# A two-layer trunk on one core: filter spectra from even and odd samples, transposes ahead of feed-forward stretches, modulation loads spread anew

## The chip, the cores and the metric

One core of one Trainium2 chip runs the whole program, in fp32. The metric is device time in microseconds (us) of one execution. TensorE (PE, with its weight loads as PEld), VectorE (DVE), ScalarE (ACT), GpSimd (POOL) and SyncE (SP, which issues nearly all DMAs here) each take their instructions in program order.

## The reference

256 latent tokens and 256 context tokens of width 2048 pass two layers. Layer 0 mixes with attention (differential and windowed heads), layer 1 with a Hyena long convolution; each is followed by a gated feed-forward with 5632 hidden columns.

```python
m = s_lat @ ada_w[l] + ada_b[l]                       # modulation: six vectors of 2048 a layer
sh1, sc1, g1, sh2, sc2, g2 = jnp.split(m, 6, axis=-1)
h = _rms(xs, norm1_g[l]) * (1.0 + sc1) + sh1
y = attention(h, hc, w_in, w_out) if l % 2 == 0 else _hyena(h, hw_in, filters, hw_out)
xs = xs + g1 * y
xs = xs + g2 * _conv_ffn(_rms(xs, norm2_g[l]) * (1.0 + sc2) + sh2, w_gate, w_val, conv_w, conv_b, w_down)

def _hyena_filters(...):                              # a small net of position: 2 orders x 2 directions x 2048
    a = jnp.sin(freq * (z @ f_w0 + f_b0)); a = jnp.sin(freq * (a @ f_w1 + f_b1)); a = jnp.sin(freq * (a @ f_w2 + f_b2))
    return (a @ f_w3).reshape(L, 2, 2, D) * decay     # the convolution then works on their spectra
```

## The kernel before

Every product of two fp32 matrices is done as three fp32r products. A weight tile of 128x2x512 fp32 (512 KB) is loaded by SP (`wload`, lines 323 to 326, a ring of six), ACT rounds it to a high part (L331), DVE subtracts to get the low part (L332, a ring of three each), and `products` (L335 to L341) issues high x high, low x high and high x low. A weight tile makes 24 matmuls of 256 columns where the activations are the moving side. `mm3` (L343 to L346) does the same for one product.

The program is one long list of stages. The start computes the first modulation vectors with PE (`ada_block`, L896 to L917, products L905), the norms of both inputs, the filter network, the filters and their spectra for the first half of the 2048 filter columns, and the first of five key/value projections. Then come the other four (KV), four query projections with attention running beside them (Q), the out-projection, feed-forward 0 (FFN0: eleven chunks of 512 hidden columns upward, each 16 weight tiles and 384 matmuls, and then two halves of eight output tiles downward), the Hyena stage, its out-projection, and FFN1.

The other modulation vectors are no PE work: class `Ada` (L454 to L498) loads a tile of 512 KB (L470, ring of six, SP) and DVE multiplies and sums it (L480). There are 320 such loads. They run in the background of the stages: `drive` (L312 to L321) calls for so many of them per step of a stage, at rates that a table of constants sets (L180 to L188), unless the flag `calm` is set. A step is one weight tile in most stages. `need` issues what is missing of a vector before its use.

Background generators do the filters in the same way: `filter_net` (L525 to L556) is the network of three layers, `filters` (L558 on) takes 512 filter columns at a time: `samples` multiplies the network's last activations by the third layer's weights (L578, plain fp32), by the decay (DVE), and sums absolute values for the normalisation; `spectra` multiplies by a table of cosines and sines in fp32r (L344 to L346) and ACT copies the result out (L604). Columns 0 to 1023 are done in the start; columns 1024 to 1535 are filling in the out-projection and in the norm's gap ahead of FFN0; the last 512 fill the second half of FFN0's down projection and the gap ahead of the Hyena stage. `GAP = 3, 5` is how many of the filling's steps are kept for the two gaps. In such a gap PE waits for a chain: sums of squares (L376), scale (L378), a Newton step on DVE and POOL (L350 to L372), a diagonal on ACT (L384), a product that spreads it (L385), and the modulated activations (L417).

## Time and profile before

| | us |
|---|---|
| three runs | 2664.08, 2691.29, 2657.86 (median 2664.08) |
| the profiled execution | 2660.88, span of its instructions 2659.0 |
| PE, PEld, DVE, ACT busy in the span | 2556.5, 2361.2, 1924.1, 1267.6 |
| first key/value stage after the start begins | 187.5 |
| FFN0 begins, its down part, the Hyena stage | 698.8, 1215.6, 1484.3 |
| FFN1 begins in earnest, ends | 1932.8, 2654.4 |

A view by windows gives, for each stretch, how long each engine was busy, the clock that TensorE was granted as a share of full speed, the busy share of the 16 DMA engines and what they moved. A row of the waits says who waited for what, for how long in total, how many times and the longest. A row of the timeline has start, duration, engine, line and operation; in brackets the idle time before it and what ended that.

### The profile page before, as it was taken

Reading aid. Unit: us, or ns where it says so; the run is one execution under the profiler, and the core shown is the slowest. Engines: PE = TensorE matmul, PEld = TensorE weight load, DVE = VectorE, ACT = ScalarE, POOL = GpSimd, SP = SyncE. Lnnn points to the kernel's source line nnn. Section 1 sums busy time; section 2 is a strip of 40 time slices with the busy share of each in tenths; the row PEclk is TensorE's granted clock in tenths of the full one; section 3 lists DMA queues with packets and bytes.
Section 4 is the critical chain, followed back from the end, with each engine's and each line's share of the span. In section 5 each row is a group of like instructions: output and inputs, shape, how many; then the busy total and the mean of one; then the engine's idle time right before and its main releaser. Section 6 shows DMA issues by size and latency. Waiting matters only on the chain.

```text
span 2659.0 us, 48167 instructions
## 1 busy us (share of the span) xinstructions
PE 2556.5 (96%) x19526; PEld 2361.2 (89%) x19526; DVE 1924.1 (72%) x2911; ACT 1267.6 (48%) x1820; POOL 37.6 (1%) x146
## 2 busy tenths in 40 slices
PE   6999998899899999999999999998999999999999
PEld 2568886678899999989999999998899999999999
DVE  5446668768898888889777678889875555556664
ACT  3452235655644443445444655554454444445543
POOL 0000000100000000000000000000000000000000
PEclk8999999999999999999999999999999999999999
DMA  8876676448799998899897665556766666666664
GB/s 293 318 267 216 213 242 232 161 151 263 242 354 327 337 342 326 316 331 344 296 309 247 202 201 170 179 176 214 253 206 193 194 193 195 194 193 196 192 211 137
DMA packets 177158, 639.99 MB, mean 241 GB/s; under 512 B 19783, under 2 KB 19880, under 8 KB 176936
## 3 DMA queue, kind: packets, MB, share of 16 engines
q1 hardware_dynamic: 174632, 628.53, 70.8%
q10 hardware_dynamic: 2304, 8.39, 0.8%
q8 instruction: 153, 2.51, 0.4%
q14 instruction: 69, 0.57, 0.1%
HBM read 624.25 MB, written 12.58 MB: 239 GB/s over the span
## 4 chain that ended last, share of the span: by engine, by line
PE 74%; DMA 9%; DVE 8%; issue 4%; ACT 4%; POOL 1%; SPq 0%; ACTq 0%; POOLq 0%; DVEq 0%
PE ps_proj L340 22%; PE ps_hy L340 9%; PE ps_kv L340 7%; PE ps_ada L340 2%; DVE araw_ada L480 2%; PE ps_q L340 1%; PE ps_ada L905 1%; DVE wlo_proj L332 1%; PE ps_attn L838 1%; PE ps_filters L578 1%; PE ps_attn L815 1%; PE ps_conv L344 1%; PE ps_conv L345 0%; PE ps_ffn1.0_3359_20701 L340 0%; PE ps_conv L346 0%
## 5 line engine op out<-in xcount | busy, mean ns | idle before, releaser
L332 DVE TENSOR_TENSOR wlo_proj<-raw_proj,whi_proj 128x1024 fp32r<-128x1024 f32 x240 | 292.3, 1221 | 145.9 <-ACT whi_proj L331 143.8
L331 ACT CAST whi_proj<-raw_proj 128x1024 fp32r<-128x1024 f32 x240 | 251.5, 1053 | 301.7 <-PE ps_proj L340 261.8
L480 DVE SCALAR_TENSOR_TENSOR araw_ada<-araw_ada,slB 128x1024 f32<-128x1024 f32 x320 | 388.9, 1217 | 0.0
L340 PE MATMUL ps_proj<-ph,whi_proj 128*128 128x256 f32 x1408 | 196.2, 279 | 0.4 <-ACT ph L349 0.3
L340 PE MATMUL ps_proj<-ph,wlo_proj 128*128 128x256 f32 x1408 | 192.9, 278 | 0.0
L340 PE MATMUL ps_proj<-pl,whi_proj 128*128 128x256 f32 x1408 | 192.8, 278 | 0.0
L340 PEld LDWEIGHTS ps_proj<-ph,whi_proj 128*128 128x128 f32 x1408 | 175.9, 188 | 4.2 <-ACT whi_proj L331 1.6
L340 PEld LDWEIGHTS ps_proj<-pl,whi_proj 128*128 128x128 f32 x1408 | 175.3, 188 | 0.0
L340 PEld LDWEIGHTS ps_proj<-ph,wlo_proj 128*128 128x128 f32 x1408 | 175.2, 188 | 0.0
L331 ACT CAST whi_hy<-raw_hy 128x1024 fp32r<-128x1024 f32 x96 | 101.3, 1056 | 105.7 <-PE ps_hy L340 82.2
L332 DVE TENSOR_TENSOR wlo_hy<-raw_hy,whi_hy 128x1024 fp32r<-128x1024 f32 x96 | 116.5, 1222 | 47.6 <-ACT whi_hy L331 46.6
L340 PE MATMUL ps_hy<-hhi,whi_hy 128*128 128x256 f32 x768 | 108.8, 281 | 1.2 <-ACT hhi L417 1.2
L340 PE MATMUL ps_hy<-hlo,whi_hy 128*128 128x256 f32 x768 | 106.0, 279 | 0.2 <-DVE hlo L419 0.2
L340 PE MATMUL ps_hy<-hhi,wlo_hy 128*128 128x256 f32 x768 | 104.5, 279 | 0.0
L340 PEld LDWEIGHTS ps_hy<-hhi,whi_hy 128*128 128x128 f32 x768 | 99.1, 189 | 3.7 <-ACT hhi L417 1.7
L340 PEld LDWEIGHTS ps_hy<-hlo,whi_hy 128*128 128x128 f32 x768 | 96.9, 188 | 1.0 <-DVE hlo L419 0.4
L340 PEld LDWEIGHTS ps_hy<-hhi,wlo_hy 128*128 128x128 f32 x768 | 95.8, 189 | 0.1
L332 DVE TENSOR_TENSOR wlo_kv<-raw_kv,whi_kv 128x1024 fp32r<-128x1024 f32 x40 | 48.8, 1222 | 60.6 <-ACT whi_kv L331 60.5
L331 ACT CAST whi_kv<-raw_kv 128x1024 fp32r<-128x1024 f32 x40 | 42.0, 1052 | 100.3 <-PE ps_kv L340 89.9
L340 PE MATMUL ps_kv<-whi_kv,hhi 128*128 128x512 f32 x256 | 66.0, 400 | 0.0
L340 PE MATMUL ps_kv<-wlo_kv,hhi 128*128 128x512 f32 x256 | 64.2, 393 | 0.0
L340 PE MATMUL ps_kv<-whi_kv,hlo 128*128 128x512 f32 x256 | 64.0, 393 | 0.0
(9816 smaller groups left out, 7652.9 us busy)
## 6 DMA issues: line engine op xcount, KB each, us to landing
araw_ada<-ada_t SPq DMA_DIRECT2D x320, 512.0 KB, 4.8
raw_proj<-wd SPq DMA_DIRECT2D x176, 512.0 KB, 4.5
raw_hy<-hw_in SPq DMA_DIRECT2D x96, 512.0 KB, 3.8
raw_ada<-ada_w SPq DMA_DIRECT2D x46, 512.0 KB, 6.6
raw_kv<-w_in SPq DMA_DIRECT2D x40, 512.0 KB, 3.8
raw_q<-w_in SPq DMA_DIRECT2D x32, 512.0 KB, 4.4
raw_proj<-w_out SPq DMA_DIRECT2D x32, 512.0 KB, 4.8
raw_proj<-hw_out SPq DMA_DIRECT2D x32, 512.0 KB, 4.5
```

The costliest lines, as they stand in the source:

```text
L331: A.copy(hi, raw)
L332: V.tensor_tensor(lo, raw, hi, op=ALU.subtract)
L340: PE.matmul(o, ll if p == 2 else lh, rl if p == 1 else rh, start=first and p == 0, stop=last and p == 2, skip_group_check=True)
L344: PE.matmul(o, lh, rh, start=first, stop=False, **kw)
L480: V.scalar_tensor_tensor(out=raw, in0=raw, scalar=1.0, in1=slB[:, h * 1024:(h + 1) * 1024], op0=ALU.mult, op1=ALU.mult, accum_out=acc[:, h ...
L578: PE.matmul(p, src[:, tt * P:(tt + 1) * P], w3[:, o], start=True, stop=True)
L815: PE.matmul(s, qT[:, h % 4, q_], KTb[:, hb // 4], start=True, stop=True)
L838: PE.matmul(o[:, 0:P], wT[:, kt * P:(kt + 1) * P], v, start=kt == 0, stop=kt == 3)
L905: PE.matmul(pv[32 * q:32 * q + 32], sl[:, 2 * i + q], raws[q // 2][:, q % 2], start=i == 0, stop=i == 6, tile_position=(0, 32 * q))
```

## The change

Five edits.

1. The cosine and sine table is halved. Samples stand in the order even, then odd; `spectra` makes one product from the even samples and one from the odd ones and gets a frequency and its mirror from their sum and difference: six matmuls of 512 columns for a half instead of twelve, one ACT copy and two DVE steps instead of two ACT copies. It yields once per half where it yielded twice.
2. `samples` uses `mm3` on the split activations and split third-layer weights (two more tiles, `w3s`) instead of an fp32 matmul.
3. In the start three steps of the filter work run before the first norm step and three behind it, the filters are stepped at 2.0 and then 1.0 instead of 1.2, and banks 2 and 3 go from the norms to the filters during the first block.
4. `turn`: four transposes of the identity into the first bank of a stretch, ahead of chunks 1 and 5 and of each down half in both feed-forwards.
5. The rates of modulation loads.

```diff
-START_RATE = 1.2
+START_RATE = 2.0, 1.0
-KV_ADA, Q_ADA, O_ADA, HY_ADA, HO_ADA = 1.3, 1.0, 0.8, 0.5, 0.6
-F0_ADA, F1_ADA = (0.9, 0.5), (0.4, 0.2)
+KV_ADA, Q_ADA, O_ADA, HY_ADA, HO_ADA = 1.9, 0.7, 0.8, 0.45, 0.6
+F0_ADA, F1_ADA = (0.7, 0.6), (0.4, 0.2)
...
+    def turn(bank):
+
+        for i in range(4):
+            PE.transpose(bank[:, i * P:(i + 1) * P], ident, ident)
...
-            a = s2([m, T]) if i < 2 else keep([P, T], "fa")
+            a = s2([m, T])
...
-        am = keep([P, T], "fam")
-        V.tensor_copy(am[:HW], a[:HW])
-        V.tensor_scalar(am[HW:], a[HW:], -1.0, None, op0=ALU.mult)
-        layers.extend((a, am))
+        for src in range(2):
+            if src:
+                V.tensor_scalar(a[HW:], a[HW:], -1.0, None, op0=ALU.mult)
+            hi, lo = (keep([P, T], f"fa{n}{src}", F32R) for n in "hl")
+            split(hi, lo, a)
+            layers.append((hi, lo))
...
-                    PE.matmul(p, src[:, tt * P:(tt + 1) * P], w3[:, o], start=True, stop=True)
+                    t = slice(tt * P, (tt + 1) * P)
+                    mm3(p, sh[:, t], sl_[:, t], w3[0][:, o], w3[1][:, o], True, True)
...
-                for f in range(2):
-                    p = ftag[0]()
-                    for tt in range(2):
-                        c = slice(half * T + f * P, half * T + (f + 1) * P)
-                        mm3(p, fh[:, tt, c], fl[:, tt, c], xh[:, tt], xl[:, tt], tt == 0, tt == 1)
-                    A.activation(so[:, f], p, AF.Copy, scale=1.0 / (2 * T))
-                    yield
+                c = slice(half * P, (half + 1) * P)
+                pe, po = ftag[0](), ftag[0]()
+                mm3(pe, fh[:, 0, c], fl[:, 0, c], xh[:, 0], xl[:, 0], True, True)
+                mm3(po, fh[:, 1, c], fl[:, 1, c], xh[:, 1], xl[:, 1], True, True)
+                e = s2([P, 512], F32, "se")
+                A.activation(e, pe, AF.Copy, scale=1.0 / (2 * T))
+                V.scalar_tensor_tensor(out=so[:, 0], in0=po, scalar=1.0 / (2 * T), in1=e, op0=ALU.mult, op1=ALU.add)
+                V.scalar_tensor_tensor(out=so[:, 1], in0=po, scalar=(half * 2 - 1) / (2 * T), in1=e, op0=ALU.mult,
+                                       op1=ALU.subtract if half else ALU.add)
+                yield
...
-            if not spare:
-                yield
+            w3s = [q4([P, 2, 512], F32R, "w3s") for _ in range(2)]
+            split(*w3s, w3)
+            yield
...
-    AD, ST = Ring(4, 5), Ring(0, 1, 2, 3)
-    ftag[0] = Ring(6, 7)
+    AD, ST = Ring(4, 5), Ring(0, 1)
+    ftag[0] = Ring(6, 7, 2, 3)
...
-    bg.one()
+    for _ in range(3):
+        bg.one()
     norm_bg.one()
+    for _ in range(3):
+        bg.one()
...
-            bg.step(START_RATE)
+            bg.step(START_RATE[g > 0])
...
             norm_bg.drain()
+            ftag[0] = Ring(6, 7)
...
                 banks = rings[half].four()
+                if n > 3:
+                    turn(banks[0])
...
             banks = ring.four()
+            if ch in (1, 5):
+                turn(banks[0])
```

Line numbers of the kernel after the change lie 8 to 23 higher: its L343 is L340 of before, L347 to L349 are L344 to L346, L384 and L393 are L376 and L385, L478 is L470, L328 is L325, L547 is L539, L920 is L905.

By stage the 320 modulation loads stand in SP's order as follows, before and after: start 2 and 5, KV 31 and 45, Q 34 and 29, with a few between the stages; out-projection 25 and 24; FFN0 up 160 and 119, FFN0 down 43 and 53; Hyena stage 1 and 2, its out-projection 15 and 14; FFN1 7 and 28.

PE's order at the beginning of the program, before: two layers of the filter network (`ps_filters`), then the first modulation products (`ps_ada`) and the sums of squares of the first norm (`ps_nx`).

```order
L539 MATMUL ps_filters_140<-s_116,u_118 64x256
L539 MATMUL ps_filters_166<-s_151,s_120 64x256
L905 MATMUL ps_ada_37_131<-raw_ada_38_132,sl 32x512 x2
L905 MATMUL ps_ada_37_131<-raw_ada_39_134,sl 32x512 x2
L376 MATMUL ps_nx_185<-ones_67,sq_153 128x1 x8
L905 MATMUL ps_ada_37_131<-raw_ada_46_158,sl 32x512 x2
L905 MATMUL ps_ada_37_131<-raw_ada_47_160,sl 32x512 x2
L539 MATMUL ps_filters_229<-s_177,s_120 128x256
```

And after the change, where `w3s` and `fah` are split parts of the third layer's weights and of the network's result:

```order
L547 MATMUL ps_filters_123<-s_116,u_118 64x256
L547 MATMUL ps_filters_136<-s_134,s_120 64x256
L547 MATMUL ps_filters_157<-s_147,s_120 128x256
L920 MATMUL ps_ada_60_195<-raw_ada_61_196,sl 32x512 x2
L920 MATMUL ps_ada_60_195<-raw_ada_62_198,sl 32x512 x2
L920 MATMUL ps_ada_60_195<-raw_ada_73_231,sl 32x512 x2
L920 MATMUL ps_ada_60_195<-raw_ada_74_233,sl 32x512 x2
L347 MATMUL ps_filters_208<-w3s_191,fah_171 128x512
```

The third layer of the network and the first samples have moved ahead of half of the first modulation products and of the first norm.

PE's order at the end of the gap ahead of FFN0, before: the last of the filling (`ps_fill`, 25 matmuls stand between the last square sum and L385), the product that spreads the norm, and the first product of FFN0.

```order
L346 MATMUL ps_fill_6001<-fhl_5661,fl_5474 128x512
L344 MATMUL ps_fill_6001<-fhl_5661,fh_5473 128x512
L345 MATMUL ps_fill_6001<-fhl_5662,fh_5473 128x512
L346 MATMUL ps_fill_6001<-fhl_5661,fl_5474 128x512
L385 MATMUL ps_proj_1288_5977<-s_5978,ones_67 128x128 x2
L340 MATMUL ps_ffn0.0_1297_6029<-hhi_6010,whi_ffn0.0_1302_6035 128x256
```

And after, where the square sums (L384) and the first group of transposes (L354) stand there:

```order
L384 MATMUL ps_proj_1312_6002<-ones_67,sq_5939 128x1
L384 MATMUL ps_proj_1312_6002<-ones_67,sq_5966 128x1
L384 MATMUL ps_proj_1312_6002<-ones_67,sq_5969 128x1
L354 MATMUL ps_ffn0.1_1392_6621<-ident_66 128x128 x4
L393 MATMUL ps_proj_1317_6030<-s_6031,ones_67 128x128 x2
L343 MATMUL ps_ffn0.0_1322_6055<-hhi_6036,whi_ffn0.0_1327_6061 128x256
```

The filling has moved ahead of the square sums, and the transposes written ahead of chunk 1 stand ahead of chunk 0. In layer 1 they stand still earlier, between the two halves of the last pass of the Hyena out-projection.

SP's order in FFN0's up part, before: a load of a modulation tile (`araw_ada`) nearly behind every weight tile (`raw_ffn0`).

```order
L325 DMA raw_ffn0.3_1518_7714<-wg 128x1024
L470 DMA araw_ada_7744<-ada_t 128x1024
L325 DMA raw_ffn0.3_1522_7747<-wv 128x1024
L470 DMA araw_ada_7777<-ada_t 128x1024
L325 DMA raw_ffn0.3_1526_7780<-wg 128x1024
L470 DMA araw_ada_7810<-ada_t 128x1024
```

And after, where some weight tiles follow each other:

```order
L328 DMA raw_ffn0.3_1541_7782<-wg 128x1024
L478 DMA araw_ada_7711<-ada_t 128x1024
L328 DMA raw_ffn0.3_1545_7815<-wv 128x1024
L328 DMA raw_ffn0.3_1550_7854<-wg 128x1024
L478 DMA araw_ada_7749<-ada_t 128x1024
L328 DMA raw_ffn0.3_1553_7884<-wv 128x1024
```

About two modulation loads have moved out for every ten weight tiles.

## Rows read from the trace of the kernel before

**Rows 1.** The page's first part: busy us and share of each engine.

```profile
PE 2556.5 (96%) x19526; PEld 2361.2 (89%) x19526; DVE 1924.1 (72%) x2911; ACT 1267.6 (48%) x1820; POOL 37.6 (1%) x146
```

**Rows 2.** Windows by stage, with the line that names the columns.

```profile
core 0: us, PE busy (x) PEld busy (x) DVE busy (x) ACT busy (x) POOL busy (x), PEclk, DMA share, GB/s
0.00:60.00 60.00, 36.36 (x137) 16.57 (x138) 33.84 (x91) 20.30 (x31) 4.62 (x26) 0.86 0.92 324
60.00:187.40 127.40, 123.05 (x589) 73.71 (x588) 55.96 (x137) 68.27 (x137) 0.00 (x0) 0.97 0.79 292
187.50:369.60 182.10, 182.10 (x811) 147.92 (x809) 111.42 (x169) 47.45 (x72) 7.01 (x30) 1.00 0.64 208
684.90:698.80 13.90, 10.78 (x56) 8.76 (x54) 9.46 (x22) 6.31 (x14) 3.78 (x10) 1.00 0.80 262
698.80:744.00 45.20, 45.20 (x384) 45.20 (x385) 42.42 (x72) 27.84 (x43) 0.00 (x0) 0.96 0.83 299
744.00:831.10 87.10, 87.10 (x771) 87.10 (x770) 77.99 (x115) 39.80 (x48) 0.00 (x0) 1.00 0.96 348
831.10:1215.60 384.50, 364.25 (x3075) 356.91 (x3074) 321.48 (x460) 161.69 (x194) 0.00 (x0) 1.00 0.92 330
1215.60:1330.30 114.70, 114.70 (x1013) 114.60 (x1012) 98.46 (x117) 64.00 (x69) 0.00 (x0) 1.00 0.89 313
1927.80:1994.20 66.40, 62.61 (x524) 62.32 (x525) 51.04 (x85) 37.73 (x59) 1.57 (x8) 0.92 0.64 206
1932.80:2654.40 721.60, 721.52 (x6336) 720.92 (x6336) 426.56 (x497) 344.71 (x412) 0.00 (x0) 1.00 0.63 192
```

**Rows 3.** Windows of line 340's matmuls on PE: us, busy (count), clock.

```profile
1220.00:1330.00 110.00, 110.00 (x973) 1.00 0.89 311
1332.00:1395.00 63.00, 63.00 (x538) 1.00 0.92 318
```

**Rows 4.** Waits of SP's queue in FFN0, 831.1 to 1215.6: us, times, longest.

```profile
SPq L470 <- DVE araw_ada L480: 238.5, 99, 5.2
```

**Rows 5.** Timeline of PE in the gap ahead of the Hyena stage.

```profile
1476.48 0.39 PE L345 MATMUL ps_fill<-fhl,fh 128*128 128x512 f32 x1
...
1478.75 0.39 PE L345 MATMUL ps_fill<-fhl,fh 128*128 128x512 f32 x1
```

**Rows 6.** Groups of PE's instructions, 0 to 190 us: the fp32 samples.

```profile
L578 PE MATMUL ps_filters<-w,fa 128*128 128x512 f32 x16 | 10.9, 768 | 3.9 <-DMA w<-f_w 3.9
L578 PE MATMUL ps_filters<-w,fam 128*128 128x512 f32 x16 | 10.5, 742 | 0.0
```

**Rows 7.** Timeline of DVE, then PE, in the gap ahead of FFN0.

```profile
689.20 1.22 DVE L480 SCALAR_TENSOR_TENSOR araw_ada<-araw_ada,slB 128x1024 f32<-128x1024 f32 x1
...
690.41 1.22 DVE L480 SCALAR_TENSOR_TENSOR araw_ada<-araw_ada,slB 128x1024 f32<-128x1024 f32 x1
...
696.88 0.78 PE L385 MATMUL ps_proj<-s,ones 128*128 128x128 f32 x4 [1.97 <-ACT s L384]
```

**Rows 8.** Timeline of PE around two groups of transposes (L1211).

```profile
1679.62 0.60 PE L1211 MATMUL ps_conv<-ident,fold 128*128 128x128 f32 x4
1679.98 1.18 PE L340 MATMUL ps_hy<-hhi,whi_hy 128*128 128x256 f32 x8
1680.99 1.07 PE L340 MATMUL ps_hy<-hlo,whi_hy 128*128 128x256 f32 x8
1681.90 1.07 PE L340 MATMUL ps_hy<-hhi,wlo_hy 128*128 128x256 f32 x8
...
1765.33 0.60 PE L1211 MATMUL ps_conv<-ident,fold 128*128 128x128 f32 x4
...
1766.71 1.11 PE L340 MATMUL ps_hy<-hlo,whi_hy 128*128 128x256 f32 x8
1767.65 1.11 PE L340 MATMUL ps_hy<-hhi,wlo_hy 128*128 128x256 f32 x8
```

**Rows 9.** The page's costliest groups: a third of the Hyena projection's products.

```profile
L340 PE MATMUL ps_hy<-hhi,whi_hy 128*128 128x256 f32 x768 | 108.8, 281 | 1.2 <-ACT hhi L417 1.2
```

More of the change, by code (lines that the diff above doesn't have):

```diff
@@ L144, in constants @@
     n = 2 * L
-    fo = np.concatenate([np.arange(0, L, 2), np.arange(1, L, 2)])[None, :]
+    fo = np.concatenate([np.arange(0, L, 2), L - 1 - np.arange(0, L, 2)])[None, :]
     t = np.arange(L)[:, None]
-    ph = np.pi * ((t * (2 * fo + 1)) % (2 * n)) / n
-    fmat = np.concatenate([np.cos(ph), np.sin(ph)], axis=1).reshape(2, P, 512).transpose(1, 0, 2).reshape(P, 1024)
+    eo = np.concatenate([np.arange(0, L, 2), np.arange(1, L, 2)])
+    ph = np.pi * ((eo[:, None] * (2 * fo[:, :P] + 1)) % (2 * n)) / n
+    fmat = np.concatenate([np.cos(ph), np.sin(ph)], axis=1).reshape(2, P, 2 * P).transpose(1, 0, 2).reshape(P, 512)
     th = np.pi * (((2 * t[:P] + 1) * (2 * fo + 1)) % (4 * n)) / (2 * n)
@@ L165, in constants @@
     return {
-        "k_tab": tab, "k_fg": fg, "k_z": np.ascontiguousarray(z.T),
-        "k_decay": np.ascontiguousarray(decay.reshape(2, P, D).transpose(1, 0, 2)),
+        "k_tab": tab, "k_fg": fg, "k_z": np.ascontiguousarray(z[eo].T),
+        "k_decay": np.ascontiguousarray(decay[eo].reshape(2, P, D).transpose(1, 0, 2)),
     }
@@ L561, in filters @@
             return
-        fh, fl = (t.rearrange("p (t f) -> p t f", t=2) for t in split_const(0, 1024, "f"))
+        fh, fl = (t.rearrange("p (t f) -> p t f", t=2) for t in split_const(0, 512, "f"))
         w3v = f_w3.rearrange("w (o d c) -> w o d c", o=2, d=2)
@@ L575, in samples @@
                 ab = []
-                for i, src in enumerate(layers):
+                for i, (sh, sl_) in enumerate(layers):
                     p = ftag[0]()
-                    PE.matmul(p, src[:, tt * P:(tt + 1) * P], w3[:, o], start=True, stop=True)
+                    t = slice(tt * P, (tt + 1) * P)
+                    mm3(p, sh[:, t], sl_[:, t], w3[0][:, o], w3[1][:, o], True, True)
                     h = s2([P, 512], F32, "hf")
@@ L617, in filters @@
             SP.dma_start(dec, k_decay[:, :, dc * 512:(dc + 1) * 512])
-            if not spare:
-                yield
+            w3s = [q4([P, 2, 512], F32R, "w3s") for _ in range(2)]
+            split(*w3s, w3)
+            yield
             for o in range(2):
                 hl = [q4([P, 2, 512], F32R, "fhl") for _ in range(4)]
-                yield from samples(o, dc, w3, dec, hl)
+                yield from samples(o, dc, w3s, dec, hl)
                 if spare and before:
@@ L1166, in trunk_kernel @@
         SP.dma_start(xsp[:, 4 * g:4 * g + 4], xs[g])
-    dh, dl = split_const(1024, 512, "d")
-    ih, il = split_const(1536, 512, "i")
+    dh, dl = split_const(512, 512, "d")
+    ih, il = split_const(1024, 512, "i")
     zb = keep([P, 48], "zb")
```

## Prediction

> **What bounds the kernel now.** The page's first part comes first: TensorE (PE) is busy 96% of the span [rows 1], so an engine average can't tell where time is to be had, and the next view is the table of windows by stage [rows 2]. Its columns are busy times per engine, the granted clock (1.00 is the 2.4 GHz level), the DMA share and GB/s. Four kinds of stage stand out. The start (0 to 187.5 us) has PE at 36.36 of its first 60 us and 123.05 of the next 127.40, with transfers at 324 and 292 GB/s: both limits are near. The KV projections run with PE at 182.10 of 182.10 us and 208 GB/s: pure PE. The up part of layer 0's feed-forward (FFN0) from chunk 3 on (831.1 to 1215.6) moves 330 GB/s at a DMA share of 0.92 with holes in PE. The whole of FFN1 (1932.8 to 2654.4) is PE at 721.52 of 721.60 us with 192 GB/s.
>
> How long would those stretches be with nothing in the way? The view of one line's matmuls [rows 3] gives it: inside an undisturbed stretch 973 products of 128x256 take 110.00 us, 113.05 ns each, and a little later, after a short stall at 1330.4, 538 take 63.00 us, 117.1 ns each, at the same clock of 1.00. So a stream has two paces, about 4.1 ns apart. FFN1's 6336 matmuls at 113.05 ns are 716.3 us of its 721.6: all quick. In FFN0 eight chunks of 384 matmuls should take 347.3 us and took 384.5, so 37.2 us are lost there. The two PE columns split them: the matmul records leave 20.3 us open, the weight loads (PEld) 27.6. I take the 27.6 as stall and the other 9.6 as the slow pace, because the end of a matmul record is modelled. The Trainium skill ("Perfetto Trace Analysis", Identifying the Most-Contended Engine) says the same of the two: pipelined matmuls make a poor measure, weight-load busy share a better one. By its rule the stall is 27.6, by matmul busy time it would be 20.3 and the sum 7 us smaller.
>
> Why the stall? A chunk takes 16 weight tiles and, at a modulation rate of 0.9 per step, 14.4 modulation loads: 30.4 tiles of 0.524 MB (15.9 MB) in 43.4 us is 367 GB/s. The best stretch of this trace moved 348, at a share of 0.96 (744 to 831.1) [rows 2]. The SP queue waits 99 times, 238.5 us in all, at the modulation load for VectorE (DVE) to free a tile [rows 4], with weight loads queued behind.
>
> **The change part by part.** Sums are made against the profiled execution, 2660.88 us (span 2659.0), which is 3.2 below the median of the runs, 2664.08.
>
> *Start.* Spectra fall from 96 to 48 matmuls of 512 columns; ten starts of such matmuls take 2.27 us (1476.48 to 1478.75) [rows 5], 0.227 each, so 10.9 us of PE go. The 16 fp32 sample products are 32 records, 10.9 + 10.5 us [rows 6], 1.34 each; three fp32r products are 0.68: at most 10.6 us go. Together 21.5 us of PE, less what lay in the holes of the first 60 us. On the other side all 56.6 MB that landed until 187.4 (324 GB/s x 60 + 292 x 127.4) need 163 us at 348 GB/s, so the start can't gain over 24. The new order puts three layers of the filter network ahead of the first modulation matmul on PE, where two stood, and samples right behind; the six weight tiles fill meanwhile and SP stops. The filter samples' own tiles are loaded ahead of the first modulation tiles (1.0 MB, 3 us). Three more modulation loads are 1.6 MB, 4.5 us of transfer. Range -4 to -20; I take **-13**, nearer to the PE row, since PE was busy 97% of the later 127 us.
>
> *KV and Q.* KV gets 45 modulation loads for 31. PE is full there, DVE idles 70.7 of 182.1 us and 14 x 1.22 us [rows 7] is 17; transfers have room at 208 GB/s. Cost **0**; if the cover failed, the price by the FFN0 rows is 27.6 us per 99 waits, 0.28 each, so +4 for 14 waits. Q gets 29 for 34: 0, at best -6 (5 x 1.22).
>
> *Fills* (filter columns 2 and 3, as filling in the out-projection, FFN0's down projection and the gaps behind them). The same saving as at the start, up to 21.5 us of PE. But two gaps are bounded by the norm's chain, and their filling was free. Of FFN0's gap (684.9 to 698.8) [rows 2] PE works 10.78 us of 13.90; the order shows 25 filling matmuls behind the last square sum there, now none, and PE will idle for most of 8 us instead. What that does to the clock is read where FFN1 starts without filling: mean clock 0.92 over 66.4 us, 5.3 us lost, against 0.96 over 45.2, 1.8, at FFN0's start: +3.5. In return two modulation products of 1.22 us that sat between the chain's small DVE steps (at 689.20 and 690.41, while PE gets its next product at 696.88) [rows 7] are gone: -2. The rest saves on the path where the projections keep PE busy: I take -6.5 of some 12. Two more tiles a column (the split third layer) must come free first; SP would wait, behind its weight ring of six. Sum **-5**, from -12 to +4.
>
> *FFN0 up.* The rate of 0.7 makes 27.2 tiles a chunk, 14.3 MB, 328 GB/s, under the 348 that has been seen and near the 313 that the down half held with no stall (1215.6 to 1330.3, PE 114.70 of 114.70) [rows 2]. Stall 27.6 falls to some 3.5: **-24**, from -10 to -27.6. The loads left go to FFN1 (28 for 7 there), where DMA stands at 0.63, and to FFN0's down part (rate 0.6, 308 GB/s wanted, seen 313).
>
> *Turns.* Eight groups of four transposes. The nearest thing before is the four transposes in the Hyena projection [rows 8]: they begin at 1679.62, the next product at 1679.98, and its first eight take 1.01 us where the following eight take 0.91. So one costs 0.36 + 0.10 = 0.46 us. One is hoisted into FFN0's gap and hidden: 7 x 0.46 = **+3.2**, from 0 to +4.
>
> *Pace of the streams.* A transposition, like a stall, lets the pace fall anew: behind the one above eight products take 0.91 us (quick), behind the one at 1765.33 0.94 (slow) [rows 8]. I counted 18 such places in the Hyena stage: 15 went on quick, 3 slow. Taking 20% slow of both layers' 12,672 products gives 10.4 us, against 9.6 in FFN0 up and 4.3 in the second down half (1056 x 4.1) before: **-3.5**, from -13.9 to +38.
>
> Sum: -13 + 0 - 5 - 24 + 3.2 - 3.5 = -42.3, so **2619 us**.
>
> **The rivals.** *The queue, not the bandwidth.* SP's waits [rows 4] say that a weight load can't be issued while the modulation load ahead of it waits for its tile; with rate 0.7 there are still 11 such loads a chunk in bursts of one. For it: 238.5 us of waits; against it: DMA share 0.92. Then the stall goes down only with the number of loads and some bursts stay: -10 in place of -24, **2633**. The Trainium skill ("HBM Reference", Specifications) gives a core that streams alone about 425 GB/s; by that 367 would fit and the queue would be the cause. No row here shows over 348.
>
> *All at its best.* Start -20, fills -12, stall -27.6, all streams quick -13.9, turns +3.2: -70, **2590**. For it: FFN1 ran quick throughout, and the down half held 313 GB/s without a hole.
>
> *Slow pace everywhere (slower).* If transposes leave the streams in the slow pace, all 12,672 products pay 4.1 ns, 52.0 us, +38 net. The same in the Hyena projection (2304 products [rows 9], about half of them slow now) adds 4.7 and the two attention and Hyena output projections (1536) 3.1. With the other terms (-13 - 5 - 24 + 3.2): +7, **2668**; it decides from about nine tenths of the products on. For it: the run of 2691.29, 30.4 above the profiled one, as if FFN1's 6336 (26 us) had run slow; against it: 15 of 18.
>
> That the change doesn't do what it says is small: the turn meant for chunk 1 stands, by the order, in FFN0's gap in layer 0 and inside the Hyena output projection in layer 1, and the rate of the Hyena stage is never used since the flag that stops loads stays set there.
>
> **How the numbers follow.** The forecast 0.50, the queue 0.18, all at its best 0.19, slow pace 0.13. A change of 2% (53 us) is about what a measurement of this kernel can tell: faster means under 2611, slower over 2717. Under 2611 lie nearly all of the best case and about a quarter of the forecast's spread: 0.31. Over 2717 only a slow pace with a start that gains nothing: 0.03. The range reaches from the best case, 2592, past the queue to 2656, before the slow case.
>
> **What would show it.** Right: KV's beginning at about 174 instead of 187.5; FFN0's chunks at 43.4 to 45 us, with the SP waits at the modulation load gone or short; the weight loads' idle time from 831 on under 5; four transposes costing 0.46 us each group; a clock under 0.96 in the first 45 us of FFN0. Wrong: chunks still at 47 us with fewer loads (the queue); products at 117 ns through FFN1 (pace); idle DMA in the first 30 us with KV beginning at 183 or later (the start).

## The result, and the profile after

The changed kernel takes 2651.73 us (median of 20 runs, 2636.50 to 2660.72) against 2662.75 (20 runs of the kernel before). The ratio is 0.9945, 95% interval 0.9926 to 0.9964: 0.6% or some 11 to 15 us faster (by the medians 11.0, by the ratio 14.6), where 2619 was forecast. The time lies inside the forecast range, the gain is a quarter to a third of the forecast one. Ratios leave out the few executions more than 1.5% above the fastest of their kernel, medians keep them. The profiled execution took 2657.26 us, its span is 2655.5, only 3.5 below the span before. Set side by side by stage (from one stage's first product to the next one's), the two spans are:

| stage | before | after | difference | forecast |
|---|---|---|---|---|
| start | 187.5 | 208.6 | +21.1 | -13 |
| KV | 182.1 | 181.6 | -0.5 | 0 |
| Q | 170.1 | 164.3 | -5.8 | 0 |
| out-projection and gap | 159.1 | 166.1 | +7.0 | part of the fills' -5 |
| FFN0 up | 516.8 | 481.0 | -35.8 | -24, and pace |
| FFN0 down and gap | 268.7 | 265.8 | -2.9 | fills, pace |
| Hyena stage, its out-projection and norm | 448.5 | 452.2 | +3.7 | |
| FFN1 and the end | 726.2 | 735.9 | +9.7 | turns and pace, about 0 in all |

So a stage that was to gain 13 us lost 21, and the stage that was to gain 24 gained 36. Each column is one execution. The last differences are not all the change's: the Hyena stage takes 447.9 to 453.7 us over the other profiles, whatever their code, and FFN0's down part with its gap 265 to 271. The windows of the changed kernel, with the columns of [rows 2], answer to the rows there:

```profile
core 0: us, PE busy (x) PEld busy (x) DVE busy (x) ACT busy (x) POOL busy (x), PEclk, DMA share, GB/s
0.00:60.00 60.00, 38.68 (x139) 19.07 (x139) 37.67 (x91) 23.69 (x38) 2.64 (x16) 0.81 0.85 293
60.00:208.50 148.50, 121.33 (x557) 75.42 (x555) 68.76 (x161) 62.93 (x126) 2.89 (x11) 0.86 0.75 268
208.60:390.20 181.60, 181.60 (x811) 147.70 (x809) 129.53 (x200) 46.99 (x71) 12.10 (x30) 1.00 0.77 258
554.50:720.60 166.10, 144.15 (x1056) 129.02 (x1056) 125.23 (x234) 80.80 (x145) 4.91 (x20) 0.96 0.60 192
708.10:720.60 12.50, 7.36 (x41) 5.82 (x39) 6.93 (x15) 4.63 (x11) 1.96 (x10) 0.70 0.48 168
720.60:765.60 45.00, 45.00 (x385) 45.00 (x386) 40.23 (x68) 27.70 (x43) 0.00 (x0) 0.97 0.75 261
852.70:1201.50 348.80, 348.80 (x3080) 348.80 (x3079) 293.76 (x410) 162.06 (x195) 0.00 (x0) 1.00 0.93 329
1919.60:2651.10 731.50, 731.37 (x6348) 730.77 (x6348) 449.13 (x538) 344.96 (x412) 0.00 (x0) 1.00 0.67 204
```

The start (first two rows) is no longer a full stage: after 60 us PE is busy 121.33 of 148.50 us where it was 123.05 of 127.40, at a mean granted clock of 0.86 for 0.97, and the transfers have fallen from 292 to 268 GB/s. No engine is full: the stage waits for something else. KV is as full of PE as before, with 258 GB/s for 208 and 129.53 us of DVE for 111.42. FFN0's chunks 3 to 10 (852.70 to 1201.50) have PE and PEld at 348.80 of 348.80: no hole is left, at a DMA share of 0.93 and 329 GB/s, the same rate as before with holes. FFN1 got slower by itself, without any hole: 731.50 us with PE at 731.37. In the gap ahead of FFN0 PE now idles for two fifths of the time (busy 7.36 of 12.50, clock 0.70); yet the gap is 1.4 us shorter than before, and FFN0's first chunk takes 45.00 us at a clock of 0.97 for 45.20 at 0.96.

SP's wait in FFN0, which answers to [rows 4], shows the same:

```profile
SPq L478 <- DVE araw_ada L488: 56.3, 73, 1.1
```

73 waits with a longest of 1.1 us, instead of 99 with a longest of 5.2: the total fell from 238.5 to 56.3 us.

FFN1's loss is the pace of [rows 3]. Line 343 (L340 before) in two stretches of it, chunks 1 to 4 and chunks 5 to 9:

```profile
1930.00:2140.00 210.00, 210.00 (x1785) 1.00 0.77 249
2160.00:2370.00 210.00, 210.00 (x1855) 1.00 0.66 194
```

210 us hold 1785 matmuls (117.6 ns each) in the first and 1855 (113.2 ns) in the second. Between them stand the four transposes of chunk 5.

### The profile page after: what moved, and what is told of

Same layout as the page of the kernel before. It is cut to its first block, busy times and chain, and to the rows that moved or that the text cites. A ratio compares the mean times of both kernels' runs of the same rounds, so it can differ in the third digit from the quotient of the medians.

```text
span 2655.5 us, 48136 instructions
## 1 busy us (share of the span) xinstructions
PE 2544.4 (96%) x19494; PEld 2364.8 (89%) x19494; DVE 1948.8 (73%) x2945; ACT 1261.4 (48%) x1807; POOL 41.9 (2%) x146
## 4 chain that ended last, share of the span: by engine, by line
PE 85%; DVE 6%; issue 3%; ACT 3%; DMA 2%; POOL 1%; SPq 0%; ACTq 0%; POOLq 0%; DVEq 0%
PE ps_proj L343 22%; PE ps_hy L343 9%; PE ps_kv L343 7%; PE ps_ada L343 2%; PE ps_q L343 1%; PE ps_ada L920 1%; DVE wlo_proj L335 1%; DMA raw_kv<-w_in 1%; PE ps_conv L347 1%; PE ps_conv L348 1%; DVE araw_ada L488 0%; PE ps_conv L349 0%; ACT whi_proj L334 0%; DMA raw_ada<-ada_w 0%; PE ps_ffn1.0_3363_20667 L343 0%
## 5 line engine op out<-in xcount | busy, mean ns | idle before, releaser
L343 PE MATMUL ps_proj<-ph,whi_proj 128*128 128x256 f32 x1408 | 192.5, 277 | 1.2 <-ACT ph L357 1.0
L343 PE MATMUL ps_proj<-pl,whi_proj 128*128 128x256 f32 x1408 | 191.5, 276 | 0.0
L343 PE MATMUL ps_proj<-ph,wlo_proj 128*128 128x256 f32 x1408 | 191.1, 276 | 0.0
L343 PEld LDWEIGHTS ps_proj<-ph,whi_proj 128*128 128x128 f32 x1408 | 174.4, 188 | 2.9 <-ACT ph L357 1.7
L343 PEld LDWEIGHTS ps_proj<-pl,whi_proj 128*128 128x128 f32 x1408 | 174.2, 188 | 0.4 <-DVE pl L358 0.3
L343 PEld LDWEIGHTS ps_proj<-ph,wlo_proj 128*128 128x128 f32 x1408 | 174.1, 188 | 0.0
L334 ACT CAST whi_hy<-raw_hy 128x1024 fp32r<-128x1024 f32 x96 | 101.2, 1055 | 108.9 <-PE ps_hy L343 85.5
L343 PE MATMUL ps_hy<-hhi,whi_hy 128*128 128x256 f32 x768 | 110.6, 284 | 1.1 <-ACT hhi L425 1.1
L343 PE MATMUL ps_hy<-hlo,whi_hy 128*128 128x256 f32 x768 | 107.3, 281 | 0.0
L343 PE MATMUL ps_hy<-hhi,wlo_hy 128*128 128x256 f32 x768 | 105.4, 280 | 0.0
L343 PEld LDWEIGHTS ps_hy<-hhi,whi_hy 128*128 128x128 f32 x768 | 100.6, 190 | 3.5 <-ACT hhi L425 1.4
L343 PEld LDWEIGHTS ps_hy<-hlo,whi_hy 128*128 128x128 f32 x768 | 98.5, 190 | 0.6
L343 PEld LDWEIGHTS ps_hy<-hhi,wlo_hy 128*128 128x128 f32 x768 | 96.8, 189 | 0.0
L343 PE MATMUL ps_kv<-whi_kv,hhi 128*128 128x512 f32 x256 | 65.9, 399 | 0.0
L343 PE MATMUL ps_kv<-wlo_kv,hhi 128*128 128x512 f32 x256 | 64.0, 391 | 0.0
L343 PE MATMUL ps_kv<-whi_kv,hlo 128*128 128x512 f32 x256 | 63.8, 391 | 0.0
```

The lines of the kernel that those rows point to most:

```text
L334: A.copy(hi, raw)
L343: PE.matmul(o, ll if p == 2 else lh, rl if p == 1 else rh, start=first and p == 0, stop=last and p == 2, skip_group_check=True)
```

## The experiments

Medians of different batches are compared by way of the kernel before, which ran beside each.

**The start, with its order put back.** Two kernels, both with everything else of the change. The first puts the whole start back, the second only the order of the first steps.

```diff
-    for _ in range(3):
-        bg.one()
+    bg.one()
     norm_bg.one()
-    for _ in range(3):
-        bg.one()
# and in the first of the two also:
-START_RATE = 2.0, 1.0
+START_RATE = 1.2, 1.2
-    AD, ST = Ring(4, 5), Ring(0, 1)
-    ftag[0] = Ring(6, 7, 2, 3)
+    AD, ST = Ring(4, 5), Ring(0, 1, 2, 3)
+    ftag[0] = Ring(6, 7)
```

> The changed kernel with the start as before: one filter step, then the first norm; filters at 1.2 a step; four banks for the norms. Halved spectra, split samples, turns and new rates stay. Theory 1 (the order: the filter steps put ahead hold the first modulation vector's copy on ACT behind the norm's chain, so the vector is ready at 48.6 us instead of 28, and SP's weight ring stands still meanwhile): the first vector's small products come again at 28 to 30 us, the KV stage at 180 to 188 us instead of 208.6, total about 2628, 22 below the changed kernel. Rival (the work itself: more splits and sums on DVE, more loads): the KV stage stays at 200 or later and the total above 2642.

> The changed kernel with only the lead undone: one filter step ahead of the first norm instead of three and three; the rates of 2.0 and 1.0 and the two banks for the norms stay. Theory 1: most of the 21 us come back, KV at 185 to 192 us. If the stepping rate of 2.0 in the first block is the cause, KV stays at 200 to 209.

With the old start the kernel takes 2628.37 us (4 runs; ratio 0.9852, interval 0.9802 to 0.9902), and KV begins at 186.8 instead of 208.6. With only the lead undone it takes 2634.05 (0.9889, 0.9824 to 0.9953), and KV begins at 191.3. So the lead is 17 of the 21 us; the other 4.5, the stepping rates and the banks, lie within the scatter of one start's code (some 7, below). Three more profiles with the lead, further below, begin KV at 204.5, 204.9 and 208.4, eight with the old start between 183.6 and 190.3. The loss stands early. The first products of the first projection, before and after:

```profile
79.76 1.09 PE L340 MATMUL ps_ada<-whi_kv,hhi 128*128 128x512 f32 x4
...
100.92 0.95 PE L343 MATMUL ps_ada<-whi_kv,hhi 128*128 128x512 f32 x3 [3.48 <-ACT whi_kv L334]
```

From there to KV it is 107.7 us in both. The timeline shows what came late. First PE of the changed kernel, where L920 are the modulation products, L384 and L393 the norm, and L927 the small products that finish the first modulation vector:

```profile
29.00 1.05 PE L920 MATMUL ps_ada<-raw_ada,sl 128*32 128x512 f32 x4
...
34.32 3.57 PE L384 MATMUL ps_nx<-ones,sq 128*128 128x1 f32 x16 [3.61 <-DVE sq L667]
...
43.15 1.23 PE L393 MATMUL ps_nx<-s,ones 128*128 128x128 f32 x4 [1.64 <-ACT s L392]
...
48.56 1.05 PE L927 MATMUL ps_ada<-sel,adast 128*128 128x2 f32 x8 [1.62 <-ACT adast L924]
```

And ACT of the changed kernel in the same stretch:

```profile
31.71 1.04 ACT L663 ACTIVATE sq<-x 128x1024 f32<-128x1024 f32 x1
42.70 0.69 ACT L392 ACTIVATE s<-ident,t 128x128 f32<-128x128 f32 x2 [9.95 <-POOL t L376]
43.30 1.64 ACT L357 CAST fhl<-hf 128x512 fp32r<-128x512 f32 x3
...
47.94 0.57 ACT L924 COPY adast<-ps_ada 128x512 f32<-128x512 f32 x1
```

The last product of the first vector starts its group at 29.00 and is done at 30.05. Its copy on ACT (L924) comes only at 47.94. Ahead of it on ACT's queue stand the squares of the first norm, which came late because filter work was put ahead of them (the square sums on PE wait until 34.32 for DVE), then the diagonal L392, which waits 9.95 us for the Newton step on POOL, and then filter work again. Before, the products and, on ACT, the copy (L909) between them stood close together:

```profile
24.31 2.98 PE L905 MATMUL ps_ada<-raw_ada,sl 128*32 128x512 f32 x16
28.03 1.05 PE L912 MATMUL ps_ada<-sel,adast 128*128 128x2 f32 x8 [0.74 <-ACT adast L909]
```

```profile
27.39 0.59 ACT L909 COPY adast<-ps_ada 128x512 f32<-128x512 f32 x1 [4.00 <-PE ps_ada L905]
```

and with the lead undone the small products come at 36.97, behind a norm whose spreading product begins at 26.21:

```profile
26.21 1.39 PE L393 MATMUL ps_nx<-s,ones 128*128 128x128 f32 x4 [1.96 <-ACT s L392]
...
36.97 0.95 PE L927 MATMUL ps_ada<-sel,adast 128*128 128x2 f32 x8
```

While the first vector hangs, the second one's loads fill SP's six tiles and stop. SP's waits for these products between 20 and 60 us, before and after:

```profile
SPq L325 <- PE ps_ada L905: 9.3, 4, 3.4
...
SPq L328 <- PE ps_ada L920: 21.1, 6, 11.5
```

From 60 to 100 us transfers then run at 216 GB/s, where they ran at 291, and the granted clock is 0.73 for 0.91, so that the PE work left there also takes longer. That the lead costs 17 us is shown by the run without it; that the copy carries them is read from the timeline. No run moved the copy alone, and none divides the loss between the wait and the clock.

**Is PE the bound of the start at all?** The kernel before, with the new rates, and with two of the three fp32r products left out of the start's spectra.

```diff
+                        if spare:
+                            PE.matmul(p, fh[:, tt, c], xh[:, tt], start=tt == 0, stop=tt == 1)
+                        else:
-                        mm3(p, fh[:, tt, c], fl[:, tt, c], xh[:, tt], xl[:, tt], tt == 0, tt == 1)
+                            mm3(p, fh[:, tt, c], fl[:, tt, c], xh[:, tt], xl[:, tt], tt == 0, tt == 1)
```

> The kernel before with the new rates, and in the start's spectra two of the three fp32r products left out (32 matmuls of 512 columns instead of 96): a pure cut of some 14.5 us of TensorE work in the start, nothing added or moved. Theory (the start is bound by transfers and by the chain through SP's ring): KV begins at 181 to 186 us, within 3 of the 183.6 of the same kernel with all products. Rival (TensorE bounds it from 60 us on): KV begins at 169 to 174.

KV begins at 187.9. The same start with all products began KV at 183.6 in one profile and at 190.3 in another, so 14.5 us of PE work less moved nothing beyond that scatter; 187.9 is above the 181 to 186 expected, but far from the rival's 169 to 174. Its window from 60 us on, to be read beside the second row of [rows 2]:

```profile
60.00:187.90 127.90, 115.58 (x523) 64.68 (x523) 57.05 (x140) 68.28 (x137) 1.05 (x1) 0.92 0.81 299
```

PE is busy 115.58 us of 127.90 for 123.05 of 127.40, and the stage is as long; transfers stay at 299 GB/s for 292. Only half of what was taken out shows in the busy time, since the granted clock fell from 0.97 to 0.92; but PE idles for 12.3 us there, so the work of PE doesn't bound the stage. What does was not tried; the trace names SP's wait for PE, in its program order, to free one of the six tiles: 95.4 us in 29 waits in the start before. In the eight other profiles with the old start KV begins between 183.6 and 190.3, whether its filter work is the old or the smaller one. The smaller one does begin the first projection earlier (68.9 to 69.7 us for 76.6 to 80.5), but these 9 us are lost again before KV.

**The rates alone**, in the kernel before.

```diff
-KV_ADA, Q_ADA, O_ADA, HY_ADA, HO_ADA = 1.3, 1.0, 0.8, 0.5, 0.6
-F0_ADA, F1_ADA = (0.9, 0.5), (0.4, 0.2)
+KV_ADA, Q_ADA, O_ADA, HY_ADA, HO_ADA = 1.9, 0.7, 0.8, 0.45, 0.6
+F0_ADA, F1_ADA = (0.7, 0.6), (0.4, 0.2)
```

> The kernel before with the five new modulation rates alone. Theory (FFN0's holes come from too many loads for the bandwidth): chunks 3 to 10 of FFN0 at 43.7 to 45.4 us instead of 47 to 50, weight-load idle time there under 3 us, total 2625 to 2632, 30 to 37 below the kernel before. Rival (the other edits also had part in it, or KV pays for its 14 more loads): a gain under 20.

2618.38 us (4 runs, 2613.91 to 2644.59; ratio 0.9847, 0.9786 to 0.9908): 41 (by the ratio) to 45 us (by the medians) faster than the kernel before it ran beside, where 30 to 37 were expected; with four runs the interval is wide. Its windows of the start from 60 us on and of chunks 3 to 10 of FFN0:

```profile
60.00:183.60 123.60, 121.03 (x583) 72.60 (x584) 52.79 (x131) 67.57 (x136) 0.00 (x0) 0.98 0.82 301
820.30:1168.60 348.30, 348.30 (x3075) 348.30 (x3075) 293.52 (x410) 161.76 (x194) 0.00 (x0) 1.00 0.93 328
```

The holes are gone (348.30 us for 384.50), with no other edit. From Q's first product to FFN0's it takes 323.2 us instead of 329.2. That is Q, by its fewer loads: it takes 162.8 to 164.5 us in all eleven profiles with the new rates and 170.1 to 171.1 in the three with the old. The start (183.6) makes most of the rest, within its scatter. KV did not pay (182.2).

**The filter edits alone**, in the kernel before, with its start order, rates and no turns (the changed kernel with all other edits undone, as in the diffs above and below).

> The kernel before with the halved spectra and the split samples alone: start, rates as before, no turns. Theory (the 20 us of TensorE work saved lie beside transfers in the start and beside chains in the gaps): KV begins at 183 to 189 us as before, FFN0 keeps its holes, total 2655 to 2670, no gain. Rival (my forecast: start -13, fills -5): 2640 to 2650.

2688.44 us (8 runs, 2665.36 to 2709.45; ratio 1.0088, 1.0050 to 1.0126): slower, which neither theory had. The start is as before (KV at 185.4). Its profile shows FFN1 at the slow pace but for the last half of its down part, 22 us; the loss apart from that lies mostly in the out-projection. First the kernel before (its stage with the gap, then the last 60 us of it), then the one with the filter edits:

```profile
539.70:698.80 159.10, 147.03 (x1070) 129.21 (x1068) 122.84 (x233) 82.38 (x149) 5.81 (x20) 1.00 0.63 200
638.60:698.80 60.20, 51.22 (x331) 42.55 (x329) 51.52 (x97) 30.12 (x54) 3.78 (x10) 1.00 0.68 221
```

```profile
540.80:711.20 170.40, 148.24 (x1055) 132.76 (x1053) 126.93 (x240) 80.94 (x146) 4.00 (x20) 0.93 0.58 190
651.00:711.20 60.20, 42.73 (x241) 37.41 (x239) 46.63 (x91) 25.89 (x48) 1.97 (x10) 0.79 0.51 170
```

The stage takes 11.3 us more, with 1055 matmuls for 1070, at a lower clock (0.93 for 1.00). In the last 60 us before, PE (51.22) and DVE (51.52) are equally busy, so these rows don't say which bounds this end of the stage. PE's waits point at DVE: for the low part of a weight tile PE waited 0.6 us before and waits 4.8 here. The edits add to DVE's work: the two sums of each spectra half, on DVE, stand where ACT copied before.

```profile
L617 DVE SCALAR_TENSOR_TENSOR spo<-ps_fill,se 128x512 f32<-128x512 f32 x4 | 2.7, 681 | 0.0
L616 DVE SCALAR_TENSOR_TENSOR spo<-ps_fill,se 128x512 f32<-128x512 f32 x4 | 2.7, 678 | 0.1
```

That is 5.4 us, and the split of the third layer another 1.2. PE saves little by the second edit. Busy times overlap, so the starts are read, in the filling of FFN0's down part, where nothing waits. An fp32 sample product (two records) among the projection's products before, then the three fp32r products of the changed kernel:

```profile
1409.48 1.02 PE L578 MATMUL ps_fill<-w,fa 128*128 128x512 f32 x2
1409.93 1.51 PE L340 MATMUL ps_proj<-ph,whi_proj 128*128 128x256 f32 x8
1411.28 1.11 PE L340 MATMUL ps_proj<-pl,whi_proj 128*128 128x256 f32 x8
1412.22 1.10 PE L340 MATMUL ps_proj<-ph,wlo_proj 128*128 128x256 f32 x8
```

```profile
1396.43 0.39 PE L347 MATMUL ps_fill<-w3s,fah 128*128 128x512 f32 x1
1396.66 0.39 PE L348 MATMUL ps_fill<-w3s,fah 128*128 128x512 f32 x1
1396.89 0.40 PE L349 MATMUL ps_fill<-w3s,fal 128*128 128x512 f32 x1
1397.13 1.07 PE L343 MATMUL ps_proj<-ph,whi_proj 128*128 128x256 f32 x8
```

From 1409.48 to 1411.28 are 1.80 us, of which the eight projection products take 0.94 (1411.28 to 1412.22): 0.86 for the fp32 product. The three fp32r products take 0.70. That is 0.16 us a product, 1.3 for the eight of a block of columns. Why the stage grows by 11.3 us here and by some 6 under the new rates (next) is open.

**The same, with DVE's share taken out again.** The version with the old start, without the work that the edits put on DVE (its spectra stay uncombined, so it serves for timing only).

```diff
-                V.scalar_tensor_tensor(out=so[:, 0], in0=po, ...)
-                V.scalar_tensor_tensor(out=so[:, 1], in0=po, ...)
+                A.activation(so[:, 0], pe, AF.Copy, scale=1.0 / (2 * T))
+                A.activation(so[:, 1], po, AF.Copy, scale=1.0 / (2 * T))
...
-            split(*w3s, w3)
+            A.copy(w3s[0], w3)
+            A.copy(w3s[1], w3)
```

> The changed kernel with the old start, and the work that the filter edits put on DVE left out: the two sums of a spectra half become two ACT copies (so the even and odd parts stay uncombined), and the low part of the split third layer is a plain ACT copy. TensorE's work is the same. Theory (the out-projection's second half is bound by DVE, and the edits' extra DVE work costs there): from the out-projection's first product to FFN0's first it takes 153 to 159 us instead of 165.2. Rival (fewer filling matmuls in the gap leave TensorE idle and at the lower clock level): 163 to 167, unchanged.

The stage and gap, in the version with the old start and then without the DVE work:

```profile
532.90:698.10 165.20, 145.35 (x1056) 130.35 (x1056) 125.06 (x234) 80.83 (x145) 4.91 (x20) 0.95 0.59 193
```

```profile
531.30:691.50 160.20, 144.10 (x1056) 128.89 (x1056) 119.66 (x225) 84.02 (x150) 4.91 (x20) 0.97 0.61 198
```

160.20 us for 165.20: 5.0 come back, just outside the 153 to 159 expected, well below the rival's 163. PE's wait for the low part goes with it; kernel before, old start, old start without the DVE work:

```profile
PE ps_proj L340 <- DVE wlo_proj L332: 0.6, 1, 0.6
...
PE ps_proj L343 <- DVE wlo_proj L335: 4.3, 4, 2.4
...
PE ps_proj L343 <- DVE wlo_proj L335: 1.3, 3, 0.6
```

Under the new rates the stage takes 157.9 to 158.9 us in the three profiles with no filter edit and 163.3 to 166.2 in the seven with all of them. So most of these 6 us are DVE's, as far as one profile of the version without the work can tell; the rest is within the scatter. Of the 5.0 us, 4.1 lie ahead of the gap (projection done 152.8 and 148.7 us after its first product).

**The turns.** The changed kernel without them, twice, and once more itself; the turns alone in the kernel before; and the old start with each group held in place.

```diff
     def turn(bank):
-        for i in range(4):
-            PE.transpose(bank[:, i * P:(i + 1) * P], ident, ident)
+        with tc.issue_after(last(PE)):
+            for i in range(4):
+                PE.transpose(bank[:, i * P:(i + 1) * P], ident, ident)
```

> The changed kernel without the eight groups of transposes. If a turn sets the quick pace (theory), some streams of FFN0 and FFN1 run at 117.8 ns for hundreds of microseconds (in one profile two or three of the eight stretches, 2 us per chunk), and the median is some 5 to 15 us above the changed kernel with a wider spread. If a turn only draws the pace anew (rival), the mean is the same within 3 us less 3.2 us of transposes.

> The changed kernel once more, beside its version without turns. If the turns cost nothing net, both medians agree within 4 us. If the turns (two of them hoisted by the scheduler) cost what the first comparison shows, it lies 8 to 12 us above.

> The changed kernel without turns once more, for the same comparison on one chip: within 4 us of the changed kernel if the turns are neutral, 8 to 12 below it if they cost. Its second down half of FFN0 slow (117.8 ns) in the profile as before.

> The kernel before with the eight groups of transposes alone, held in place. Theory (a turn sets the quick pace, 28 of 28 so far): every product stream directly behind a turn at 113.3 ns until the next hole, the second down half of FFN0 quick (down part 3 us shorter), FFN0's holes untouched; total within 5 us of before, the runs' spread smaller since FFN1 can no longer run slow. Rival (drawn anew): some of the eight at 117.8 ns.

> The start as before, and each group of transposes held in place behind the instruction written ahead of it, so that the two meant for chunk 1 stand there. Theory (turn sets the quick pace): chunks 1 to 4 of FFN1 at 43.7 us in the profile whatever chunk 0 does, total 2615 to 2625, the spread of the runs narrower than the changed kernel's 24 us. Rival (pace drawn anew, 15 of 18 quick): one of the eight stretches slow in the profile, total about 2630.

Without turns: 2641.22 (10 runs; ratio 0.9906, 0.9878 to 0.9933), and again 2645.29 (10 runs; 0.9943, 0.9905 to 0.9980). The changed kernel once more, on the same chip as the second: 2653.26 (10 runs; 0.9945, 0.9910 to 0.9979). The ratios of the direct comparison agree, but the medians lie 8.0 us apart, which was to be the mark of a cost, and runs of one kernel scatter by some 30 us: a cost of up to some 10 us, or a gain, is not told from nothing. The expected loss without turns of 5 to 15 us didn't come. The 20 runs without turns form two groups, 15 between 2637.13 and 2647.69 and 5 between 2659.26 and 2667.65. A profile of each group was taken: with FFN1 at the quick pace in the one, at the slow one up to the last half of its down part in the other.

The turns alone in the kernel before: 2665.92 (10 runs; 0.9999, 0.9968 to 1.0029), no change. In that profile chunks 1 to 4 of FFN1 run quick behind a turn, and chunks 5 on run slow behind the next:

```profile
1990.00:2140.00 150.00, 150.00 (x1326) 1.00 0.64 194
2160.00:2400.00 240.00, 240.00 (x2040) 1.00 0.62 186
```

150 us hold 1326 (113.1 ns), 240 us hold 2040 (117.6 ns). So the theory that a turn always sets the quick pace fell. Over the eight profiles with turns 54 of them stand in their place, and 51 are followed by the quick pace. Most stretches were quick already; the eight turns behind a slow stretch tell more, and all eight are followed by the quick pace. At the same three places of FFN1 without turns, in the two profiles where it runs slow, the pace stayed slow four times in six. One of the eight, in the changed kernel's FFN1 (behind the turn's 0.36 us the first two products start 0.21 us apart instead of 0.113):

```profile
2148.25 0.60 PE L354 MATMUL ps_ffn1.5_3680_23333<-ident 128*128 128x128 f32 x4
2148.61 0.37 PE L343 MATMUL ps_ffn1.5_3680_23333<-hhi,whi_ffn1.5_3685_23343 128*128 128x256 f32 x1
2148.82 0.28 PE L343 MATMUL ps_ffn1.5_3681_23334<-hhi,whi_ffn1.5_3685_23343 128*128 128x256 f32 x1
```

The two that the scheduler moves do nothing for chunk 1. The one of layer 1 stands here, in the Hyena out-projection, 24 us before FFN1 begins:

```profile
1895.58 0.60 PE L354 MATMUL ps_ffn1.1_3429_21221<-ident 128*128 128x128 f32 x4
1896.51 0.50 PE L343 MATMUL ps_proj<-h2h,whi_proj 128*128 128x256 f32 x2 [0.33 <-ACT whi_proj L334]
```

Held in place, with the old start: 2622.37 (4 runs; 0.9838, 0.9782 to 0.9893), and all streams behind the eight turns quick in its profile.

**Rates and turns in place, nothing else**, in the kernel before.

> The kernel before with the new modulation rates and the eight groups of transposes held in place, nothing else. Theory (the rates are the whole gain, the turns only keep the pace quick, 38 of 40 so far): median 2614 to 2622, and no run near 2644, where the rates alone had one of four. Rival (the filter edits also gain something, the start aside): slower than the version with all edits and the old start, that is above 2625.

2623.45 (6 runs, 2620.62 to 2632.11; ratio 0.9856, 0.9830 to 0.9883), just above the range expected; its profile has the latest start of all with the old order, 190.3. The spread is narrow, as expected. Against the version with the filter edits (2622.37) no difference shows: under the new rates the filter edits are worth nothing that can be told from the noise, which is some 15 us in that run's interval.

So the fastest versions all lie between 2618 and 2624, too close to rank: the new rates alone, with the turns held in place, or with these and the filter edits behind the old start.

## Why the prediction was wrong, point by point

*The start.* -13 was forecast, +21.1 came. The step that failed is "I take -13, nearer to the PE row, since PE was busy 97% of the later 127 us". Taking 14.5 us of PE work out of the start moved KV by nothing beyond the scatter, and so did the smaller filter work behind the old start (184.0 to 186.8): a full engine there was not the bound. What bounds the start instead is open; SP's wait for its six tiles is the candidate that the trace names. The other number of that step, 56.6 MB at 348 GB/s, is no firm floor either: from 20 to 40 us the kernel before moved 377, and from 10 to 20 us 413. The saving was also too large: by the starts above an fp32 product gives back 0.16 us and not 0.66, so 16 of them give 2.6 us where up to 10.6 were counted. And the range of the term (-4 to -20) had no end above nothing, though the order showed the network's third layer ahead of the first modulation products and the samples ahead of half of them, and the text says that SP stops there. The price that was left out is that of the lead, 17 us: by the timeline it holds up a copy on ACT behind a norm's chain, at 47.94 instead of 27.39 us.

*FFN0 up.* Right in what it changes, small in size: -24 for the stall and about -6 for the pace, against 35.7 in chunks 3 to 10, of the 37.2 that [rows 2, 3] give as lost. I left 3.5 us of stall and counted a fifth of the products slow; there were none of either in this profile (in the second one of the changed kernel chunks 0 to 4 of FFN0 ran at 117.8 ns, so the pace was luck). The rates alone closed the holes (348.30 us), so the cause is the number of loads. The rival of the queue is refuted in its size, -10: with the loads thinned the waits and the holes left together, and 329 GB/s were moved in both. Whether bandwidth or the queue made the holes isn't settled by that, since fewer loads ease both. "The best stretch of this trace moved 348" was wrong (377 and 413, above), though these were short.

*KV and Q.* KV 0, as forecast, under 258 GB/s. Q: 0 taken, -5.8 came, the end of the range (-6). This and the surplus of FFN0 hid part of the start's loss; that the time lies in the range is owed to them.

*Fills.* -5 forecast, +7 in the out-projection of the changed kernel. The term failed where it says "The rest saves on the path where the projections keep PE busy": at that end of the stage PE waits for DVE, and the edits add 6.6 us of DVE work for each block of columns. The saving itself was priced too high here too, by the busy time of overlapping records. The price set on the lost cover (+3.5) did not come: the clock fell to 0.70 in the gap and PE idled for 5 us of it, but the gap got no longer (12.50 us for 13.90 before and 12.8 with the new rates alone) and FFN0's start no slower. The loss lies ahead of the gap, 153.6 us for 145.2.

*Turns and pace.* 0.46 us a turn fits the one above (0.36 and 0.09 on the next product). The pace behind them is quick more often than the 15 of 18 counted, 51 of 54. But two are moved away, and the first chunks of FFN1 are left to chance: 9.9 us of the profiled execution, its three turns included. That these are runs' chances and not the change's shows in the kernel without turns, whose runs fall in two groups some 24 us apart.

*The signs that were named.* Right: FFN0's chunks (43.6 us), SP's short waits (1.1), no idle time of the weight loads from 831 on, the cost of a turn. Wrong: KV at 208.6 and not 174, and the clock in FFN0's first 45 us (0.97, not under 0.96). The idle transfers that were to betray the start in its first 30 us came later: the DMA share is 0.94 in the first 30 us and 0.61 from 60 to 100.

*The balance.* Rates -38 to -45, the start's order +15 to +25, the filter edits nothing to some +7 under the new rates, the turns about nothing: these ends take in the -11 to -15 that were measured. Under the old rates the filter edits cost some 23 us; how much of it is the pace, which was slow in the one profile, is open. What the scatter of the start (183.6 to 190.3 for the same code) comes from wasn't tried.

## What to carry to other kernels

An engine that is busy 97% of a stage need not be what the stage waits for: before pricing work taken off it, ask what the stage would wait for without it, and take some work out as a test. When background work is moved ahead, follow each in-order queue for the small step that the next loads hang on; here moving it cost 17 us, and the timeline shows a copy of 0.6 us held behind a norm's diagonal. And spread background loads out of the stages that want the most: here 367 GB/s wanted left holes and 328 left none, and that alone was worth more than the whole change.

## What was not expected of the hardware

Identical product streams have two paces at a granted clock of 1.00 (113.2 and 117.6 ns), kept for hundreds of microseconds until something interrupts the stream; in FFN1 that makes some 24 us between two groups of executions of the same program. Four transposes in between were followed by the quick one 51 times in 54, and eight times in eight behind a slow stretch; why, no run here shows. And some 329 GB/s were moved both with holes in PE and without: the rate moved didn't tell the two apart, the rate wanted (367 and 328) did.
